# A layer norm queued two to four gate pieces sooner, half of its sums of squares on VectorE, and two output rows interleaved by weight half

## The chip, the cores and the metric

One core of one Trainium2 chip runs the whole program. The metric is the device time of one execution in microseconds (us), as the median of several runs. A profiled execution gives a trace with a record of each instruction on each engine. The engines are called PE (TensorE, the matrix engine), DVE (VectorE), ACT (ScalarE), POOL (GpSimd) and SP (SyncE, which here only issues transfers).

## The reference

The reference is one step of a streaming encoder with two layers, for a prompt of 1024 frames and 8 running streams of 16 frames each: 1152 rows of 1024 numbers, in float32. Layer 0 is attention beside a spatial gate. Layer 1, where the change lies, is this (shortened):

```
def _conv_layer(x, conv_state, norm_g, w_in, w_dw, b_dw, ln_g, ln_b, w_out):
    xn = _rmsnorm(x, norm_g)
    z = jnp.einsum('btd,de->bte', xn, w_in)
    a, b, g = jnp.split(z, [C_WIDTH, 2 * C_WIDTH], axis=-1)
    u = a * jax.nn.sigmoid(b)
    ctx = ...                       # u behind 30 earlier rows
    c = lax.conv_general_dilated(ctx, w_dw, ...) + b_dw        # depthwise, 31 taps
    c = jax.nn.silu(_layernorm(c, ln_g, ln_b)) * jax.nn.silu(g)
    y = x + jnp.einsum('btc,cd->btd', c, w_out)
    return y, ctx[:, -(CONV_WIDTH - 1):]
```

`_layernorm` subtracts the mean over the 1024 channels, divides by the root of the variance, scales and shifts. After layer 1 a last RMS norm with `final_g` gives the outputs `y_prompt` (1024 rows) and `y_sample` (128 rows).

## The kernel before

Every float32 product is made of three matmuls: each operand is split into a high part and the rest (`wh`, `wl` for weights, `yh`, `yl` for the normed input, `ch`, `cl` for the layer's result), and `mm3` (L157) adds high by high, high by rest and rest by high. `split_w` splits a piece of weights of 128x1024: a load into `raw` on SP's queue, a cast to `wh` on ACT (L145), and a subtraction to `wl` on DVE, or on the engine given as `low` (L146).

In `phase_conv` channels lie on the partitions and the 1152 rows (tokens) along the free side. Eight arrays `cT[0..7]`, each 128x1152, hold the convolution's result for 128 channels each. Most conv tiles go through memory: the result is stored in `s_c`, loaded into a `big` buffer, and copied into `cT[i]` with the bias by DVE (L1217 and L1220, inside `back`). `back` also adds up `msum`, the sum of `cT[0]` to `cT[6]`.

After the conv tiles come eight gate tiles i (0 to 7, 128 gate channels each). A gate tile has three column pieces c of 384 tokens. A piece is 24 matmuls of 128x384 (8 channel blocks by 3), then a silu on ACT into `sg[i]` (L980). Below, the pieces are numbered 3i + c, from 0 to 23.

The layer norm runs beside the gate tiles, for one column piece c at a time, in three steps:

- `norm_sum` (L1009 to L1020): two matmuls with a matrix `ones` add the channels of `msum` and `cT[7]`; ACT writes the mean into `msum` (L1011); for each of the eight blocks DVE subtracts it (L1014), ACT squares (L1016) into a buffer, and POOL adds the square to one of two sums, `ac0` and `ac1` (L1020). The squares of blocks 0 and 1 are the sums' first values; the other six go through two buffers, `sq`, used in turn.
- `norm_var` (L1028 to L1034): six narrow matmuls add each of the sums over the channels; DVE and POOL make the inverse root (L125, L126); DVE writes it on diagonals (L1034).
- `norm_apply` (L1041 to L1045): a matmul spreads it over the partitions, ACT copies it into `msum` (L1042); for each block DVE multiplies (L1044) and ACT applies scale, shift and silu (L1045).

`LN_STEPS` gives for each c the pieces behind whose last matmul these three steps are issued. The order within each engine's queue is set by the program's scheduler, which simulates the program as it is written; `issue_after` ties a step to an instruction. `ones` is written by a memset on DVE (L1002) after `back(7)`.

Behind the gate tiles DVE multiplies `cT` by `sg` (L1064, 24 operations). Then w_out's product runs over nine tiles t of 128 rows. For each tile ACT casts `ch2` from the eight `cT` (L1079), DVE subtracts to `cl2` (L1080), and PE makes two products of 24 matmuls of 128x512, one for each half of w_out's columns; DVE adds each to `x`, and a norm writes the rows out. The first half of w_out's weights is split beside the last gate tiles (the list `wo`), the second half at the start of the last stage. PE runs its queue strictly in order.

Of the kernel before, what the change touches and what calls it, by code (L numbers as in the profile page):

```python
# [11 lines left out]
F32 = mybir.dt.float32  # L12
F32R = mybir.dt.float32r
AF = mybir.ActivationFunctionType
ALU = mybir.AluOpType
# [4 lines left out]
P = 128  # L20
# [5 lines left out]
NT = 9  # L26
# [68 lines left out]
BACK = 3  # L95
HPT = 400
TAIL = 1
LN_STEPS = ((10, 13, 15), (13, 16, 18), (16, 19, 21))
LAST = (7, 4, 6, 3, 5, 2, 1, 0)
QB = 4  # L100
GB = 3
# [3 lines left out]
class Builder:  # L105
# [809 lines left out]
    def phase_conv(self):  # L915
        nc, tc, a = self.nc, self.tc, self.a
        with ExitStack() as st:
            E = st.enter_context
            pm = E(tc.tile_pool(name="pm2", bufs=3, space=PSUM, reuse_waits="tile"))
# [10 lines left out]
            cT = [cp.tile([P, TOK], F32, name=f"cT{i}") for i in range(8)]  # L930
# [42 lines left out]
            def gate_tile(i, wb):  # L973
                i2 = i % 2
                for c in range(3):
                    ts_ = slice(c * 384, (c + 1) * 384)
                    ps = pm.tile([P, 512], F32, name="mm")
                    last = self.mm3(ps[:, :384], [(x[:, i2 * P:(i2 + 1) * P], y[:, i2 * P:(i2 + 1) * P]) for x, y in wb],
                                    self.yk(c))
                    nc.scalar.activation(sg[i][:, ts_], ps[:, :384], AF.Silu)  # L980
# [24 lines left out]
            def norm_sum(c):  # L1005
                ts_ = slice(c * 384, (c + 1) * 384)
                mu = msum[:, ts_]
                ps = pl.tile([P, 512], F32, name="ln")
                nc.tensor.matmul(ps[:, :384], lhsT=ones, rhs=mu, start=True, stop=False)  # L1009
                nc.tensor.matmul(ps[:, :384], lhsT=ones, rhs=cT[7][:, ts_], start=False, stop=True)  # L1010
                nc.scalar.activation(mu, ps[:, :384], AF.Copy, scale=1.0 / D)  # L1011
                acc = [None, None]
                for i in range(8):
                    nc.vector.tensor_tensor(cT[i][:, ts_], cT[i][:, ts_], mu, ALU.subtract)  # L1014
                    sq = wk.tile([P, 384], F32, name="sq" if i > 1 else f"ac{i}", bufs=2 if i > 1 else 1)
                    nc.scalar.activation(sq, cT[i][:, ts_], AF.Square)  # L1016
                    if i < 2:
                        acc[i] = sq
                    else:
                        nc.gpsimd.tensor_tensor(acc[i % 2], acc[i % 2], sq, ALU.add)  # L1020
                ln[c] = acc

            def norm_var(c):
# [28 lines left out]
            for j in range(1, 4):  # L1052
                wb = self.split_w(wp, [a["w_in1"][:, 2 * D + j * 256:2 * D + (j + 1) * 256]], 256)
                for i2 in range(2):
                    i = 2 * j + i2
# [2 lines left out]
                        wo = [self.split_w(wp, [a["w_out1"][:, :512]], 512, p) for p in range(2)]  # L1058
            wo += [self.split_w(wp, [a["w_out1"][:, :512]], 512, p) for p in (2, 3)]
            wb = [sum(wo, [])]  # L1060
            for c in range(3):
                ts_ = slice(c * 384, (c + 1) * 384)
                for i in range(8):
                    nc.vector.tensor_tensor(cT[i][:, ts_], cT[i][:, ts_], sg[i][:, ts_], ALU.mult)  # L1064
            s3.close()
            s4.close()
            self.xstack.close()
            with ExitStack() as s2:
                wp4 = s2.enter_context(tc.tile_pool(name="wp4", bufs=4, side="right", reuse_waits="tile"))
# [4 lines left out]
                for t in range(NT):  # L1074
                    ts_ = slice(t * P, (t + 1) * P)
                    ch = wk.tile([P, 8, P], F32R, name="ch2")
                    cl = wk.tile([P, 8, P], F32R, name="cl2")
                    for i in range(8):
                        nc.scalar.copy(ch[:, i], cT[i][:, ts_])  # L1079
# [3 lines left out]
                    for i in range(2):  # L1083
                        ps = pm.tile([P, 512], F32, name="mm")
                        self.mm3(ps, [(ch[:, k], cl[:, k]) for k in range(8)], wb[i])
                        nc.vector.tensor_tensor(x[:, i * 512:(i + 1) * 512], x[:, i * 512:(i + 1) * 512], ps, ALU.add)
                    yo = wk.tile([P, D], F32, name="yo")
                    if t == NT - 1:
                        self.norm_out(a["y_sample"].rearrange("b q d -> (b q) d"), yo, x, gb)
                        continue  # L1090
                    self.norm(yo, x, gb)
                    nc.sync.dma_start(out=a["y_prompt"][0, ts_, :], in_=yo)
            self.wstack.close()

    def conv_tile(self, i, wb, pm, ub, cv, chan, wdw, scr, same, hooks, late):
# [154 lines left out]
```

## Time and profile before

| | |
|---|---|
| median of 3 runs | 1223.09 us (1223.04 to 1224.46) |
| profiled execution | 1223.68 us, span 1221.9 us |
| mean granted clock of PE | 0.979 of full speed |
| ACT busy | 456.8 us (37%), 1065 instructions |
| POOL busy | 340.7 us (28%), 510 instructions |
| gate pieces 7 to 23 and norm steps | about 1027 to 1108 us |
| last gate matmul begins | 1108.18 us |
| first w_out matmul begins | 1113.00 us |

Times in the trace count from the span's start. The profiled execution's own time is 1.8 us longer than its span. Busy time counts an engine's instructions and not its waits; a record's length can be longer than the slot that it takes, since an engine begins an instruction before the one ahead has ended. What a stretch costs is read from starts.

### The profile page before, as it was taken

To read this page: it belongs to the slowest core of one execution; us is meant where nothing else is said; L and a number is where in the kernel's file an instruction comes from. 1 tells how busy PE (TensorE), PEld (TensorE's weight loads), DVE (VectorE), ACT (ScalarE), POOL (GpSimd) and SP (SyncE) were. 2 spreads that over 40 slices of the span, in tenths; PEclk is the share of its full clock that TensorE was granted. 3 is DMA by queue.
4 is the path that set the end of the run, shared out by engine and by line. 5 is a ranking of instruction groups with operands and counts; after the bars stand their busy time and mean duration, and the time that the engine had idled before them with its cause. 6 is when DMAs were issued, how large, how long until landed. Compare 5 with 4: busy or idle time off the path is not lost. (4 is left out here: it accounts for less than half of the span.)

```text
span 1221.9 us, 20908 instructions
## 1 busy us (share of the span) xinstructions
PE 1156.0 (95%) x7886; PEld 1024.1 (84%) x7886; DVE 731.6 (60%) x1560; ACT 456.8 (37%) x1065; POOL 340.7 (28%) x510
## 2 busy tenths in 40 slices
PE   6999999999989998679999999999999999998997
PEld 4878998899989997457777677899999899996886
DVE  4420225678788878766556444698999711377443
ACT  4431223445454545555444334312121222365221
POOL 2233223334434435413322231212131220350000
PEclk9999999999989998879999999999999999998999
DMA  8453435324132313867767635333332442113331
GB/s 302 110 169 91 144 118 172 107 71 121 46 89 78 108 50 105 301 214 242 258 226 255 192 125 190 92 91 96 93 96 90 140 134 84 35 35 104 104 104 69
DMA packets 125365, 160.33 MB, mean 131 GB/s; under 512 B 16514, under 2 KB 87194, under 8 KB 125257
## 3 DMA queue, kind: packets, MB, share of 16 engines
q1 hardware_dynamic: 109344, 106.95, 28.5%
q0 software_dynamic: 15776, 51.79, 12.9%
q8 instruction: 62, 1.02, 0.3%
q14 instruction: 39, 0.31, 0.1%
q10 hardware_dynamic: 144, 0.26, 0.1%
HBM read 119.41 MB, written 40.00 MB: 130 GB/s over the span
## 5 line engine op out<-in xcount | busy, mean ns | idle before, releaser
L157 PE MATMUL mm<-yh,wh 128*128 128x384 f32 x576 | 196.5, 341 | 3.3 <-ACT sb L1133 2.5
L157 PE MATMUL mm<-yl,wh 128*128 128x384 f32 x576 | 193.9, 337 | 0.5 <-issue 0.5
L157 PE MATMUL mm<-yh,wl 128*128 128x384 f32 x576 | 193.8, 338 | 0.3 <-DVE wl L146 0.2
L157 PE MATMUL mm<-wh,xh 128*128 128x384 f32 (+1 forms) x504 | 185.4, 369 | 2.5 <-DVE sg L468 1.4
L157 PE MATMUL mm<-wl,xh 128*128 128x384 f32 (+1 forms) x504 | 184.5, 366 | 0.9 <-DVE wl L146 0.9
L157 PE MATMUL mm<-wh,xl 128*128 128x384 f32 (+1 forms) x504 | 183.7, 364 | 0.0
L146 DVE TENSOR_TENSOR wl<-raw,wh 128x1024 fp32r<-128x1024 f32 (+1 forms) x72 | 84.3, 1178 | 104.7 <-ACT wh L145 102.7
L1173 DVE SCALAR_TENSOR_TENSOR cT<-u,cc,cT 128x128 f32<-128x128 f32 (+1 forms) x180 | 141.3, 843 | 1.0
L157 PEld LDWEIGHTS mm<-yh,wh 128*128 128x128 f32 x576 | 108.7, 189 | 6.2 <-issue 2.8
L157 PEld LDWEIGHTS mm<-yh,wl 128*128 128x128 f32 x576 | 108.6, 189 | 2.0 <-DVE wl L146 0.9
L157 PEld LDWEIGHTS mm<-yl,wh 128*128 128x128 f32 x576 | 108.7, 189 | 1.1 <-issue 0.7
L157 PEld LDWEIGHTS mm<-wh,xh 128*128 128x128 f32 x504 | 95.7, 190 | 13.3 <-DVE sg L468 1.4
L157 PEld LDWEIGHTS mm<-wl,xh 128*128 128x128 f32 x504 | 95.9, 190 | 10.5 <-DVE wl L146 1.8
L157 PEld LDWEIGHTS mm<-wh,xl 128*128 128x128 f32 x504 | 95.7, 190 | 8.7 <-DVE xl L170 0.3
L145 ACT CAST wh<-raw 128x1024 fp32r<-128x1024 f32 (+1 forms) x72 | 71.8, 1001 | 73.0 <-PE mm L157 30.9
L126 POOL TENSOR_TENSOR rr<-pw,mhalf 128x1 f32<-128x1 f32 x59 | 33.0, 559 | 200.3 <-DVE pw L125 190.8
L559 ACT ACTIVATE e<-S,nm 128x512 f32<-128x512 f32 (+5 forms) x96 | 55.1, 579 | 42.1 <-DVE nm L554 26.4
L157 PE MATMUL out<-wh,ch 128*128 128x512 f32 x144 | 59.9, 416 | 2.0 <-DVE xr L845 1.2
L157 PE MATMUL mm<-wh,ch 128*128 128x512 f32 x144 | 57.1, 397 | 4.5 <-ACT ch L1079 4.5
L551 DVE TENSOR_REDUCE nm<-S 128x1 f32<-128x512 f32 (+5 forms) x96 | 52.5, 551 | 12.6 <-PE S L546 11.9
L777 DVE TENSOR_TENSOR vl<-vraw,vh 128x1024 fp32r<-128x1024 f32 x32 | 43.2, 1351 | 26.8 <-ACT vh L776 26.6
L157 PE MATMUL out<-wh,cl 128*128 128x512 f32 x144 | 58.8, 408 | 0.0
(282 smaller groups left out, 2300.6 us busy)
## 6 DMA issues: line engine op xcount, KB each, us to landing
raw<-in_cache_k SPq DMA_DIRECT2D x32, 512.0 KB, 4.4
vraw<-in_cache_v POOLq DMA_DIRECT2D x32, 512.0 KB, 5.7
raw<-in_w_in SPq DMA_DIRECT2D x24, 512.0 KB, 5.3
raw<-in_w_out SPq DMA_DIRECT2D x16, 512.0 KB, 5.0
raw<-in_w_in SPq DMA_DIRECT2D x32, 256.0 KB, 4.0
raw<-in_w_in SPq DMA_DIRECT2D x48, 128.0 KB, 2.8
s_y<-xr POOLq DMA_DIRECT2D x9, 512.0 KB, 4.7
x<-s_y SPq DMA_DIRECT2D x9, 512.0 KB, 4.3
```

The lines of the kernel that those rows point to most:

```text
L126: m = nc.gpsimd.tensor_tensor(out, v[:, :w], self.mhalf[:, :w], ALU.pow)
L145: nc.scalar.copy(h[:, :ks * n], raw[:, :ks * n])
L146: (low or nc.vector).tensor_tensor(l[:, :ks * n], raw[:, :ks * n], h[:, :ks * n].bitcast(F32), ALU.subtract)
L157: m = self.nc.tensor.matmul(out, lhsT=x, rhs=y, start=(i == 0), stop=(i == n - 1))
L551: nc.vector.tensor_reduce(nm[:, j:j + 1], s[:, :n], AX.X, ALU.max, negate=True)
L559: nc.scalar.activation(e[:, j * n:(j + 1) * n], S[j][:, :n], AF.Exp, bias=nv, accum_out=zz[:, j:j + 1])
L777: (nc.vector if i in VDVE else nc.gpsimd).tensor_tensor(vl, vr, vh.bitcast(F32), ALU.subtract)
L1173: nc.vector.scalar_tensor_tensor(dst, src, w1, dst, ALU.mult, ALU.add)
```

## The change

There are four edits. The layer norm's steps are issued behind earlier pieces. The sums of squares of odd blocks (`ac1`) are added on DVE. The multiplication by `sg` moves into gate tile 7, behind each of its pieces. In the last stage the second half's splits have their subtraction on POOL and are issued ahead of the load of `final_g`, and the products of rows 0 and 1 run in the order (0, first half), (1, first half), (0, second half), (1, second half).

```diff
-LN_STEPS = ((10, 13, 15), (13, 16, 18), (16, 19, 21))
+LN_STEPS = ((6, 9, 11), (10, 13, 15), (14, 17, 19))
...
                     with tc.issue_after(last):
                         for f in (hooks_of(8) if i < 2 else steps).get(3 * i + c, ()):
                             f()
+                    if i == 7:
+                        for k in range(8):
+                            nc.vector.tensor_tensor(cT[k][:, ts_], cT[k][:, ts_], sg[k][:, ts_], ALU.mult)
...
-                        nc.gpsimd.tensor_tensor(acc[i % 2], acc[i % 2], sq, ALU.add)
+                        (nc.vector if i % 2 else nc.gpsimd).tensor_tensor(acc[i % 2], acc[i % 2], sq, ALU.add)
...
-            for c in range(3):
-                ts_ = slice(c * 384, (c + 1) * 384)
-                for i in range(8):
-                    nc.vector.tensor_tensor(cT[i][:, ts_], cT[i][:, ts_], sg[i][:, ts_], ALU.mult)
...
+                wb.append(self.split_w(wp4, [a["w_out1"][:, 512:]], 512, low=nc.gpsimd))
                 nc.sync.dma_start(out=gb, in_=a["final_g"].partition_broadcast(P))
-                wb.append(self.split_w(wp4, [a["w_out1"][:, 512:]], 512))
...
+                rows_in(0)
+                rows_in(1)
+                for t, i in ((0, 0), (1, 0), (0, 1), (1, 1)):
+                    product(t, i)
+                rows_out(0)
+                rows_out(1)
+                for t in range(2, NT):
+                    rows_in(t)
+                    for i in range(2):
+                        product(t, i)
+                    rows_out(t)
```

`rows_in` holds the old loop's casts, subtractions and load of `x` for one tile, `product` one product and its addition to `x`, `rows_out` the norm and the store. The new lines shift the numbers: L1009, L1020 and L1044 of before are L1012, L1023 and L1047 after, and so on; the multiplication by `sg` is L986 (before L1064).

PE's queue around the first `norm_sum`. Before, its pair of matmuls stands between pieces 10 (tile 3, c = 1) and 11 (`yh1` and `yh2` are the normed input of columns 1 and 2; a name in brackets with a number, as in DVE_49, is a semaphore that the instruction waits for):

```order
L157 MATMUL mm_11255<-yl1_8100,wh_11147 128x384
L157 MATMUL mm_11255<-yh1_8099,wl_11148 128x384
L1009 MATMUL ln_11281<-msum_8270,ones_11137 128x384 [waits DVE_49,PE_49]
L1010 MATMUL ln_11281<-cT7_8269,ones_11137 128x384
L157 MATMUL mm_11315<-yh2_7982,wh_11141 128x384 [waits Activation_49]
```

and after, inside piece 7 (tile 2, c = 1), behind eleven of its matmuls:

```order
L157 MATMUL mm_11211<-yh1_8099,wh_11141 128x384 [waits Activation_49]
L157 MATMUL mm_11211<-yl1_8100,wh_11141 128x384
L157 MATMUL mm_11211<-yh1_8099,wl_11142 128x384
...
L157 MATMUL mm_11211<-yh1_8099,wh_11141 128x384
L157 MATMUL mm_11211<-yl1_8100,wh_11141 128x384
L1012 MATMUL ln_11177<-msum_8270,ones_11137 128x384 [waits DVE_49,Activation_49]
L1013 MATMUL ln_11177<-cT7_8269,ones_11137 128x384
L157 MATMUL mm_11211<-yh1_8099,wl_11142 128x384
```

The pair has moved up by three and a half pieces. DVE's queue ahead of the subtractions has the same order in both: here it is after the change.

```order
L146 TENSOR_TENSOR wl_11412<-raw_11409,wh_11411 128x1024 [waits PE_49,Activation_49]
L1236 TENSOR_SCALAR cT7_8269<-big_11089,cc_8271 128x1024 [waits DMAHW6_49]
L1239 TENSOR_SCALAR cT7_8269<-big_11089,cc_8271 128x8x8 x2
L146 TENSOR_TENSOR wl_11418<-raw_11415,wh_11417 128x1024 [waits DMAHW5_49,PE_49,Activation_49]
L1005 MEMSET ones_11137 128x128 [waits DMAHW1_49,Pool_49]
L1017 TENSOR_TENSOR cT0_8262<-cT0_8262,msum_8270 128x384 [waits DVE_49,Activation_49]
```

The memset of `ones`, on which L1012 waits, is still the last of these before the subtractions.

DVE's queue from the second column's `norm_sum` on, after the change (L1017 subtracts the mean, L1023 is DVE's share of the sums, L1047 belongs to the first column's `norm_apply`):

```order
L1017 TENSOR_TENSOR cT7_8269<-cT7_8269,msum_8270 128x384 [waits PE_49]
L146 TENSOR_TENSOR wl_11551<-raw_11548,wh_11550 128x1024 [waits PE_49,Activation_49]
L146 TENSOR_TENSOR wl_11557<-raw_11554,wh_11556 128x1024 [waits DMAHW7_49,PE_49,Activation_49]
L1023 TENSOR_TENSOR ac1_11338<-ac1_11338,sq_11345 128x384 [waits Activation_49]
L1047 TENSOR_TENSOR cT0_8262<-cT0_8262,msum_8270 128x384 [waits Activation_49]
L1047 TENSOR_TENSOR cT1_8263<-cT1_8263,msum_8270 128x384
L1047 TENSOR_TENSOR cT2_8264<-cT2_8264,msum_8270 128x384
...
L1047 TENSOR_TENSOR cT7_8269<-cT7_8269,msum_8270 128x384
L1023 TENSOR_TENSOR ac1_11338<-ac1_11338,sq_11353 128x384 [waits Activation_49]
```

Before, the same multiplications (of the third column's sums, L1044) stand like this:

```order
L1044 TENSOR_TENSOR cT0_8262<-cT0_8262,msum_8270 128x384 [waits DVE_49,Activation_49]
L1044 TENSOR_TENSOR cT1_8263<-cT1_8263,msum_8270 128x384 [waits DVE_49]
L1044 TENSOR_TENSOR cT2_8264<-cT2_8264,msum_8270 128x384 [waits DVE_49]
L1044 TENSOR_TENSOR cT3_8265<-cT3_8265,msum_8270 128x384 [waits DVE_49]
L1044 TENSOR_TENSOR cT4_8266<-cT4_8266,msum_8270 128x384 [waits DVE_49]
```

The multiplications have moved into the second column's sums, and their wait for a semaphore of DVE's own is gone.

ACT's queue at the end of the gate tiles, before the change:

```order
L145 CAST wh_11867<-raw_11865 128x1024 [waits DMAHW3_49,PE_49]
L1045 ACTIVATE cT5_8267<-cT5_8267,cc_8271 128x384 [waits DVE_49]
L980 ACTIVATE sg7_11133<-mm_11833 128x384 [waits PE_49]
L145 CAST wh_11908<-raw_11906 128x1024 [waits DMAHW4_49]
L1079 CAST ch2_11930<-cT0_8262 128x128
```

and after it:

```order
L1048 ACTIVATE cT7_8269<-cT7_8269,cc_8271 128x384 [waits DVE_49]
L980 ACTIVATE sg7_11133<-mm_11781 128x384 [waits PE_49]
L980 ACTIVATE sg7_11133<-mm_11815 128x384 [waits PE_49]
L145 CAST wh_11885<-raw_11883 128x1024 [waits DMAHW2_49,PE_49,Activation_49]
L145 CAST wh_11891<-raw_11889 128x1024 [waits DMAHW3_49,PE_49,Activation_49]
L980 ACTIVATE sg7_11133<-mm_11849 128x384 [waits PE_49]
L145 CAST wh_11907<-raw_11905 128x1024 [waits DMAHW4_49]
L1080 CAST ch2_11930<-cT0_8262 128x128
```

The last `norm_apply` (L1048) has moved ahead of gate tile 7's first silu (L980); the two casts of weights around the last silu stand where they stood.

More of the change, by code (lines that the diff above doesn't have):

```diff
@@ L1071, in phase_conv, with rows_in @@
                 gb = wk.tile([P, D], F32, name="gb", bufs=1)
+                wb.append(self.split_w(wp4, [a["w_out1"][:, 512:]], 512, low=nc.gpsimd))
                 nc.sync.dma_start(out=gb, in_=a["final_g"].partition_broadcast(P))
[L1073 to L1074 removed]
+                rows = {}
+                def rows_in(t):
                     ts_ = slice(t * P, (t + 1) * P)
@@ L1082, in phase_conv, with product, rows_out @@
                     nc.sync.dma_start(out=x, in_=self.s_y1[ts_, :])
[L1083 to L1086, printed above, removed]
+                    rows[t] = ch, cl, x
+                def product(t, i):
+                    ch, cl, x = rows[t]
+                    ps = pm.tile([P, 512], F32, name="mm")
+                    self.mm3(ps, [(ch[:, k], cl[:, k]) for k in range(8)], wb[i])
+                    nc.vector.tensor_tensor(x[:, i * 512:(i + 1) * 512], x[:, i * 512:(i + 1) * 512], ps, ALU.add)
+                def rows_out(t):
+                    x = rows[t][2]
                     yo = wk.tile([P, D], F32, name="yo")
```

4 lines of the change are left out of this document (2 added, 2 removed).

## Prediction

> **What bounds the kernel.** First the page's table of busy time, then the waits of the matrix engine (PE) after 1000 us, which is where everything in the change lies, and then the last pieces of the chain that ended last (start, length, what).
>
> ```profile
> PE 1156.0 (95%) x7886; PEld 1024.1 (84%) x7886; DVE 731.6 (60%) x1560; ACT 456.8 (37%) x1065; POOL 340.7 (28%) x510
> ...
> PE mm L157 <- ACT ch L1079: 4.5, 1, 4.5
> PE mm L157 <- DVE wl L146: 0.7, 1, 0.7
> ...
> 1115.36 99.09 PE mm L157 x429
> ```
>
> PE is busy 95% of the span, and the chain's last long piece is PE's alone. So a microsecond that PE stands still after 1000 us comes out as a microsecond of the end, and work of the other engines costs nothing while PE has matmuls. Between 1000 us and the last gate matmul PE waits for no engine; its waits are both at the seam where the gate tiles end and the w_out product begins. So the change can gain only at that seam, and can lose wherever the earlier steps make PE wait. The seam comes next: PE's records (start, us, line, tile, and in brackets the idle time before), then windows (length, PE busy, instructions, granted clock, DMA share, GB/s).
>
> ```profile
> 1108.18 0.34 PE L157 MATMUL mm<-yh,wl 128*128 128x384 f32 x1
> 1113.00 0.79 PE L157 MATMUL mm<-wh,ch 128*128 128x512 f32 x1 [4.48 <-ACT ch L1079]
> ...
> 1118.83 0.39 PE L157 MATMUL mm<-wh,ch 128*128 128x512 f32 x1
> 1119.05 0.39 PE L157 MATMUL mm<-wl,ch 128*128 128x512 f32 x1
> ...
> 1108.44:1111.86 3.42, 0.08 (x1) 1.00 0.66 213
> 1111.86:1115.27 3.41, 1.65 (x3) 0.50 0.72 263
> 1115.27:1118.68 3.41, 3.32 (x8) 0.50 0.81 263
> 1118.68:1122.10 3.42, 3.42 (x17) 1.00 0.08 31
> ```
>
> The last gate matmul's slot ends at 1108.36 (0.17 a slot). Eleven matmuls start from 1113.00 to before 1118.83 (x3 and x8 in the windows). At full clock, from 1118.83 on, one takes a slot of 0.227 (0.39 is its own length, which overlaps the next). So 10.5 us from 1108.36 to 1118.83 did work of 11 slots, 2.5 us. The seam loses 8.0 us. Two things make it: idle time, 5.2 us, and two windows at half clock, which follow a window in which PE did almost nothing.
>
> **The clock's price.** The granted clock changes on a grid of 3.41 us. Two earlier places show what it takes.
>
> ```profile
> 492.64 0.66 PE L417 MATMUL tr<-cst,raw 128*128 128x128 f32 x4 [2.21 <-DVE KT L418]
> ...
> 490.63:494.04 3.41, 1.05 (x7) 1.00 0.86 310
> 494.04:497.46 3.42, 3.42 (x18) 0.50 0.75 238
> 975.32:978.73 3.41, 1.81 (x84) 1.00 0.45 159
> 978.73:982.14 3.41, 3.41 (x107) 1.00 0.02 5
> ```
>
> A window with PE busy for 0.31 of it was followed by one at half clock; one with 0.53 was not. I take one half as the limit. A half-clock window costs 1.7 us, half of its length. So a gap of over 1.7 us can cost its length and 1.7 more, if it falls into one window.
>
> **Part A, norm_sum of the first column piece, four gate pieces sooner.** In the new order its two matmuls over `ones` stand behind 11 matmuls of gate piece 7 instead of behind piece 10. They wait for VectorE (DVE), whose queue ahead of them has not moved: the copies of the last conv tile (L1217, L1220), a weight split, and then the memset of `ones`.
>
> ```profile
> 1029.71 1.20 DVE L1217 TENSOR_SCALAR cT<-big,cc 128x1024 f32<-128x1024 f32 x1 [6.29 <-DMA big<-s_c]
> 1030.84 0.44 DVE L1220 TENSOR_SCALAR cT<-big,cc 128x64 f32<-128x64 f32 x2
> 1031.21 1.21 DVE L146 TENSOR_TENSOR wl<-raw,wh 128x1024 fp32r<-128x1024 f32 x1
> 1032.39 0.17 DVE L1002 MEMSET ones<- 128x128 f32 x1
> ...
> 1027.32 0.33 PE L157 MATMUL mm<-yh,wh 128*128 128x384 f32 x1
> ...
> 1029.22 0.33 PE L157 MATMUL mm<-yh,wl 128*128 128x384 f32 x1
> ```
>
> 1027.32 is piece 7's first matmul; 11 slots later, at 1029.23, PE reaches the moved pair. The memset ends at 1032.56, because the DMA that feeds L1217 lands at 1029.71. PE therefore stands 3.3 us. That DMA hangs on the convolution, which the change does not touch, and behind the pair PE's whole gate work is queued in order. The clock: the grid (1108.44 less 23 windows) has an edge at 1029.9, so of the window to 1033.35 PE works some 0.8 us, under a quarter; the next is at half clock, 1.7. If the grid lies otherwise, two windows may share the gap and neither falls. Part A costs 3.3 to 5.0; I take 5.0.
>
> **Part B, the sums of squares.** Of the 18 additions nine go from POOL to DVE. On DVE one costs a slot of 0.48 (eight L1014 in 3.84 below). Nine are 4.3 us, and four weight splits of 1.15 leave DVE, both beside PE work. What matters is how POOL fares beside DVE. Here are POOL's additions and one small power operation, with what DVE did meanwhile.
>
> ```profile
> 1049.01 3.94 POOL L1020 TENSOR_TENSOR ac<-ac,sq 128x384 f32<-128x384 f32 x1 [46.64 <-ACT sq L1016]
> ...
> 1049.26 0.55 DVE L1014 TENSOR_TENSOR cT<-cT,msum 128x384 f32<-128x384 f32 x1
> 1049.73 2.35 DVE L146 TENSOR_TENSOR wl<-raw,wh 128x1024 fp32r<-128x1024 f32 x2
> ...
> 1052.92 3.92 POOL L1020 TENSOR_TENSOR ac<-ac,sq 128x384 f32<-128x384 f32 x4
> ...
> 1080.70 3.83 DVE L1014 TENSOR_TENSOR cT<-cT,msum 128x384 f32<-128x384 f32 x8
> 1080.86 4.39 POOL L126 TENSOR_TENSOR nm<-pw,mhalf 128x3 f32<-128x3 f32 x1 [6.39 <-DVE pw L125]
> ...
> 1071.37 1.33 POOL L1020 TENSOR_TENSOR ac<-ac,sq 128x384 f32<-128x384 f32 x1
> ...
> 1070.65 2.47 DVE L1044 TENSOR_TENSOR cT<-cT,msum 128x384 f32<-128x384 f32 x2 [5.11 <-ACT msum L1042]
> ```
>
> An addition alone takes 0.98 (four in 3.92). The one at 1049.01 took 3.94 and ended 0.9 after DVE's run of two-input operations ended at 1052.08: it had not begun before. The power operation likewise waited out eight L1014. At 1071, beside L1044, it was otherwise: POOL's addition took 1.33 and two L1044 took 2.47 instead of 1.2, so they alternated. The difference in the program is that each L1044 waits for a semaphore of DVE's own, and L1014 and the splits do not. In the new order the multiplications (now L1047) carry no such wait either, as the L1014 of before. So a run of them shuts POOL out.
>
> For the second column piece DVE's queue is then one such run: eight subtractions, two splits, one addition, eight multiplications of the first column's norm_apply, 3.8 + 2.3 + 0.5 + 3.8 = 10.4 us. POOL's first addition of that column is asked for inside it.
>
> ```profile
> 1043.96 0.81 PE L1009 MATMUL ln<-msum,ones 128*128 128x384 f32 x2
> 1044.60 0.81 PE L1010 MATMUL ln<-cT,ones 128*128 128x384 f32 x2
> ...
> 1045.97 3.84 DVE L1014 TENSOR_TENSOR cT<-cT,msum 128x384 f32<-128x384 f32 x8 [13.42 <-ACT msum L1011]
> 1046.62 0.52 ACT L1016 ACTIVATE ac<-cT 128x384 f32<-128x384 f32 x1 [0.69 <-DVE cT L1014]
> ```
>
> From norm_sum's first matmul: DVE begins after 2.0 (1045.97 less 1043.96), its run ends after 12.4, POOL's first addition after 13.3. The two `sq` buffers make the later squares wait for it, so square, addition, square, addition follow: 2 x (0.52 + 0.98), after 16.3, and 0.2 for the hand-overs. PE comes to norm_var after 72 gate matmuls of 0.173 and three wide matmuls of 0.64, 14.4. It stands 2.1 us; the clock's 1.7 comes with it about three times in five, and I take it: 3.8. The bounds: POOL gets in early and nothing is lost, 0; or POOL's third addition too is shut out by the gate multiplications that now follow in DVE's queue, another 2, so 5.8.
>
> The Trainium skill ("SBUF — State Buffer", section "SBUF: two separate sides") says that VectorE's two-input operations and GpSimd share one port pair as a lock, which whoever starts first holds for one instruction. By it POOL would get in at the next instruction's end, and the sum would lack B (the first rival). The rows of 1.33 and 2.47 agree with that, those of 3.94 and 4.39 do not: there POOL waited out two to eight instructions.
>
> **Part C, the third column.** Its last addition now stands on DVE behind seven multiplications (7 x 0.47 = 3.3) with the split that opens the last gate tiles behind it; PE waits for both. The square that it needs comes late itself, so I take 0.5, between 0 and 3.3.
>
> **The seam after the change.** All norm_apply steps and nearly all gate multiplications (L986, before L1064) are over by the last gate matmul. ScalarE (ACT) still has in its queue a weight cast whose buffer the last gate piece frees, the last silu, a second cast, and then the first `ch2` cast, for which PE waits.
>
> ```profile
> 1109.80 1.03 ACT L145 CAST wh<-raw 128x1024 fp32r<-128x1024 f32 x1
> ...
> 1111.35 0.47 ACT L980 ACTIVATE sg<-mm 128x384 f32<-128x384 f32 x1
> 1111.72 1.03 ACT L145 CAST wh<-raw 128x1024 fp32r<-128x1024 f32 x1
> 1112.65 0.70 ACT L1079 CAST ch<-cT 128x128 fp32r<-128x128 f32 x3
> ```
>
> Slots of 0.94 + 0.37 + 0.93 and a cast of 0.3: 2.6 us idle (5.2 before). One window, not two, then runs at half clock: 1.7. The seam loses 4.3 instead of 8.0, a gain of 3.7; 5.4 if the clock holds, 8.0 if the seam closes. Interleaving rows 0 and 1 puts 48 matmuls (10.9 us) ahead of the first use of w_out's second half, so its four splits, now on POOL, are hidden even at 2.4 us each, the length of an operation of that size there:
>
> ```profile
> L180 POOL TENSOR_TENSOR yn<-yn,gb 128x1024 f32<-128x1024 f32 x8 | 19.1, 2392 | 10.1 <-ACT yn L179 10.1
> ```
>
> The swapped loads on SP's queue and the second `x` load land long before the additions after 24 matmuls. The norm of row 0 comes later, beside row 2's product: nothing. The end after the last matmul does not change.
>
> **Sum.** 5.0 + 3.8 + 0.5 - 3.7 = +5.6 on the profiled execution's 1223.68, 1229.3. That execution lies 0.59 above the median of the runs, 1223.09, so 1228.7.
>
> **Rivals.** First: POOL gets in between DVE's operations, B is 0. For it speak the rows at 1071; against it those at 1049 and 1080, whose unmarked operations are the kind that the new order has. 5.0 + 0.5 - 3.7 = +1.8: 1224.9. Chance 0.19.
>
> Second, the other side: the seam closes wholly, because the casts come early enough that `ch2` is ready by the last gate matmul. It decides if ACT has the first cast done at the slot's end; then 8.0 is gained, and with B and C at nothing 5.0 - 8.0 = -3.0, 1220.1. Against it: the cast that waits for the last gate matmul stands ahead of `ch2` in ACT's queue. Chance 0.08.
>
> Third: the gaps of 2 to 3 us never lower the clock. 3.3 + 2.1 + 0.5 - 5.4 = +0.5: 1223.6. The row with 2.21 idle at 492.64 and its half-clock window speak against it. Chance 0.08. The Trainium skill ("TensorE: Matmul & The Clock Gate", section "Why this matters for your kernels") warns only of PE gaps over some 3 us, which would give this rival's time; the trace's clock fell with a gap of 2.21.
>
> Fourth: at the seam POOL's first split takes the port before the `cl2` subtractions, and PE's third matmul waits out most of its 2.4: 2.2 more, 1230.9. For it: POOL's split is asked for before the `cl` of row 0. Chance 0.12.
>
> **Chances and range.** My forecast, A and B with the smaller seam, has 0.53; its own range is 1227 (B without the clock) to 1231 (a longer B). Within 0.2% of the median (2.45 us, about what a measurement here can tell from no change) lie the first rival, near the edge, and the third; faster is the second. With a little of the first over the edge: faster 0.08, same 0.24, slower 0.68. The range takes the first, third and fourth in and reaches to B's upper bound: 1223.0 to 1233.0.
>
> **What would show it.** A: a wait of L1012 for DVE of about 3.3 near 1029, then a window at 0.50. B: a POOL addition of several us at about 1056 to 1064, ending just after DVE's multiplications, and PE's L1031 waiting about 2 for POOL near 1067. The seam: 2.6 idle before the first w_out matmul, released by `ch2`, and one window at half clock. I am wrong if `ones` is there by 1029, if POOL's additions all stay near 1.0 to 1.4, or if the seam's wait is gone.

## The result, and the profile after

The changed kernel is slower: 1230.45 us median (1229.41 to 1233.0, 6 runs) against 1223.66 for the kernel before on the same chip, a ratio of 1.0056 with a 95% interval of 1.0044 to 1.0069. The forecast was 1228.7, in a range of 1223.0 to 1233.0. The profiled execution took 1229.75 us with a span of 1228.0, 6.1 more than the span before.

PE's waits after 1000 us (line, who was waited for, total, times, longest), of the changed kernel:

```profile
PE ln L1012 <- DVE ones L1005: 3.4, 1, 3.4
PE mm L157 <- ACT ch L1080: 2.5, 1, 2.5
PE ln L1031 <- POOL ac L1023: 1.9, 1, 1.9
PE mm L157 <- DVE cl L1081: 1.9, 1, 1.9
PE ln L1032 <- DVE ac L1023: 0.5, 1, 0.5
PE mm L157 <- DVE wl L146: 0.3, 1, 0.3
```

The busy shares of the page say nothing: they are the same within a point (PE 94% of the span after 95%). The waits say more. Before there were two, at the seam, of 5.2 us. Now there are six, of 10.5 us, and the first, third, fifth and sixth stand in the gate tiles, where PE had not waited for any engine.

The two stages can be read from three records of PE in each trace: the first matmul of gate piece 7, the last gate matmul, and the last matmul of w_out. For the changed kernel:

```profile
1026.52 0.33 PE L157 MATMUL mm<-yh,wh 128*128 128x384 f32 x1
...
1115.74 0.34 PE L157 MATMUL mm<-yh,wl 128*128 128x384 f32 x1
...
1220.11 0.39 PE L157 MATMUL mm<-wh,cl 128*128 128x512 f32 x1
```

From piece 7 to the last gate matmul are 89.22 us (before: 1108.18 less 1027.32, 80.86), a loss of 8.4. From there to the last matmul are 104.4 us (105.9 before), a gain of 1.5. Piece 7 itself began 0.8 earlier, which has nothing to do with the change. 8.4 - 1.5 - 0.8 gives the 6.1 of the span. So the two stages together lost 6.9, and 0.8 of it was made up by chance.

The first wait. DVE's rows, and PE's:

```profile
1029.07 1.11 DVE L1236 TENSOR_SCALAR cT<-big,cc 128x1024 f32<-128x1024 f32 x1 [6.45 <-DMA big<-s_c]
1030.46 1.22 DVE L146 TENSOR_TENSOR wl<-raw,wh 128x1024 fp32r<-128x1024 f32 x1
1031.65 0.17 DVE L1005 MEMSET ones<- 128x128 f32 x1
...
1031.96 1.26 PE L1012 MATMUL ln<-msum,ones 128*128 128x384 f32 x2 [3.37 <-DVE ones L1005]
...
1028.89:1032.30 3.41, 0.34 (x1) 1.00 0.07 28
1032.30:1035.71 3.41, 3.41 (x9) 0.51 0.50 156
```

PE stands from 1028.6 until the memset is done; a window with PE busy for a tenth is followed by one at half clock.

The second column's sums, DVE and POOL and then PE:

```profile
1053.12 3.84 DVE L1017 TENSOR_TENSOR cT<-cT,msum 128x384 f32<-128x384 f32 x8 [3.75 <-ACT msum L1014]
1056.87 2.36 DVE L146 TENSOR_TENSOR wl<-raw,wh 128x1024 fp32r<-128x1024 f32 x2
1059.14 0.56 DVE L1023 TENSOR_TENSOR ac<-ac,sq 128x384 f32<-128x384 f32 x1
1059.61 3.84 DVE L1047 TENSOR_TENSOR cT<-cT,msum 128x384 f32<-128x384 f32 x8
...
1056.20 8.12 POOL L1023 TENSOR_TENSOR ac<-ac,sq 128x384 f32<-128x384 f32 x1 [7.54 <-issue]
1064.95 1.01 POOL L1023 TENSOR_TENSOR ac<-ac,sq 128x384 f32<-128x384 f32 x1 [0.63 <-ACT sq L1019]
...
1067.64 0.38 PE L1031 MATMUL ln<-ones,ac 128*128 128x1 f32 x2 [1.92 <-POOL ac L1023]
...
1063.02:1066.43 3.41, 2.69 (x16) 1.00 0.04 14
1066.43:1069.85 3.42, 2.21 (x13) 1.00 0.01 2
```

DVE runs without a gap from 1053.12 to 1063.45. POOL's addition is on record as 8.12 us long and busy; it ends 0.9 after the run. An addition alone takes 1.01, in the next row. The clock did not fall: the gap lies across the edge of two windows, which are 0.79 and 0.65 busy.

The seam:

```profile
1118.60 0.50 PE L157 MATMUL mm<-wh,ch 128*128 128x512 f32 x1 [2.52 <-ACT ch L1080]
1121.17 0.79 PE L157 MATMUL mm<-wh,cl 128*128 128x512 f32 x1 [1.85 <-DVE cl L1081]
...
1118.42 2.54 POOL L146 TENSOR_TENSOR wl<-raw,wh 128x1024 fp32r<-128x1024 f32 x1 [22.86 <-ACT wh L145]
1118.67 5.48 DVE L1081 TENSOR_TENSOR cl<-cT,ch 128x128 fp32r<-128x128 f32 x16
...
1121.05:1124.46 3.41, 3.29 (x8) 0.50 1.03 398
```

POOL's first split began 0.25 before DVE's `cl2` subtractions and lasted until 1120.96; PE's first matmul over `cl` began 0.2 later. So the seam has 2.5 idle for `ch2`, 1.85 for `cl2` and one half-clock window of 1.7, some 6 us. The stage gained 1.5 on the 8.0 of before, which puts the loss at 6.5.

### The profile page after: what moved, and what is told of

It reads as the page before. It is cut to its first block, busy times and chain, and to the rows that moved or that the text cites. A ratio compares the mean times of both kernels' runs of the same rounds, so it can differ in the third digit from the quotient of the medians.

```text
span 1228.0 us, 20895 instructions
## 1 busy us (share of the span) xinstructions
PE 1157.6 (94%) x7886; PEld 1025.7 (84%) x7886; DVE 734.8 (60%) x1565; ACT 456.0 (37%) x1065; POOL 342.1 (28%) x505
## 5 line engine op out<-in xcount | busy, mean ns | idle before, releaser
L146 DVE TENSOR_TENSOR wl<-raw,wh 128x1024 fp32r<-128x1024 f32 (+1 forms) x68 | 79.6, 1176 | 105.3 <-ACT wh L145 102.7
L157 PEld LDWEIGHTS mm<-wl,xh 128*128 128x128 f32 x504 | 96.3, 191 | 10.5 <-DVE wl L146 1.8
```

The source lines that it names most:

```text
L146: (low or nc.vector).tensor_tensor(l[:, :ks * n], raw[:, :ks * n], h[:, :ks * n].bitcast(F32), ALU.subtract)
L157: m = self.nc.tensor.matmul(out, lhsT=x, rhs=y, start=(i == 0), stop=(i == n - 1))
```

## The experiments

All times of stages come from the three PE records named above, one profiled execution each. The ratio is that of the runs to those of the kernel before on the same chip, with its 95% interval. The start of piece 7 moved between 1025.5 and 1033.7 from one execution to the next (e9 aside, whose first wait stands ahead of it), on code that no kernel here changes, so the stages are the sharper measure. They hold the half-clock windows that the execution happened to have, some 1.7 us each, so the table gives their number, with PE's waits in the gate stage.

| kernel | gate, us | of it waits | w_out, us | half-clock windows, gate and w_out | ratio to before |
|---|---|---|---|---|---|
| before | 80.9 | 0 | 105.9 | 0, 2 | 1 |
| the change | 89.2 | 6.2 | 104.4 | 1, 1 | 1.0056 [1.0044, 1.0069] |
| e1: first column at 8, 10, 12 | 81.9 | 1.0 | 105.4 | 0, 2 | 1.0000 [0.9985, 1.0015] |
| e2: multiplications read PSUM | 87.0 | 4.4 | 105.3 | 1, 2 | 1.0058 [1.0036, 1.0080] |
| e3: second half split on DVE | 90.5 | 5.9 | 103.3 | 2, 1 | 1.0043 [1.0025, 1.0061] |
| e4: all sums on POOL | 94.1 | 6.6 | 104.2 | 4, 1 | 1.0077 [1.0057, 1.0098] |
| e5: old steps | 85.7 | 3.1 | 104.8 | 1, 2 | 1.0030 [1.0011, 1.0049] |
| e6: all sums on DVE | 88.7 | 4.8 | 105.5 | 2, 2 | 1.0040 [1.0019, 1.0061] |
| e7: rows not interleaved | 91.9 | 5.7 | 104.0 | 3, 1 | 1.0080 [1.0055, 1.0105] |
| e8: better steps, all on DVE | 80.5 | 0 | 102.3 | 0, 1 | 0.9956 [0.9940, 0.9973] |
| e9: `ones` written early | 91.5 | 5.3 | 104.2 | 3, 1 | 1.0051 [1.0032, 1.0071] |
| e10: the steps alone | 96.4 | 7.0 | 102.9 | 5, 1 | 1.0091 [1.0062, 1.0120] |
| e11: e8 with half the sums on POOL | 80.4 | 0 | 102.0 | 0, 1 | 0.9941 [0.9922, 0.9960] |

In every row the gate stage is the 80.9 of before, PE's waits and 1.7 for each half-clock window, within 0.5 us. So no larger cost is hidden in that stage. The gate stage of the change, e3 and e7 is the same code with nearly the same waits; its 89.2, 90.5 and 91.9 differ by their one, two and three half-clock windows. A difference of one or two windows between single profiles therefore need not be an effect of an edit. The intervals of e2, e3, e4, e5, e6, e7, e9 and e10 all overlap that of the change. So the runs alone tell these kernels from the change barely or not at all, and what is said of them below rests on the waits in their profiles.

The main theory is that of the prediction: two stalls in the gate tiles that the earlier steps make (one for `ones`, one for POOL shut out by DVE), and a smaller gain at the seam. The main rival is that the work moved to DVE makes the loss.

### e1: the first column two pieces later

```diff
-LN_STEPS = ((6, 9, 11), (10, 13, 15), (14, 17, 19))
+LN_STEPS = ((8, 10, 12), (10, 13, 15), (14, 17, 19))
```

> The changed kernel with the first column's steps behind pieces 8, 10 and 12 instead of 6, 9 and 11. Theory (two stalls and the seam): norm_sum now reaches PE after the memset of ones (about 1031.8), so the 3.4 us wait of L1012 and its half-clock window (1.7) are gone, 5.1; in return norm_var of the second column comes to PE earlier against POOL, whose addition stays shut out, so L1031's wait for POOL grows from 1.9 to about 3 and may cost a half-clock window. Net 2 to 4 us faster than the changed kernel, about 1227. Rival (the extra work on VectorE makes the loss, the wait for ones is covered by later slack): within 1 us of the changed kernel, 1230.

PE's waits of e1, then POOL's first addition of the second column with what DVE did:

```profile
PE mm L157 <- ACT ch L1080: 2.5, 1, 2.5
PE mm L157 <- DVE cl L1081: 1.9, 1, 1.9
PE ln L1032 <- DVE ac L1023: 1.0, 1, 1.0
...
1059.48 2.25 POOL L1023 TENSOR_TENSOR ac<-ac,sq 128x384 f32<-128x384 f32 x1 [4.19 <-issue]
...
1059.66 1.22 DVE L146 TENSOR_TENSOR wl<-raw,wh 128x1024 fp32r<-128x1024 f32 x1
1062.32 0.56 DVE L1023 TENSOR_TENSOR ac<-ac,sq 128x384 f32<-128x384 f32 x1 [1.44 <-ACT sq L1019]
```

The wait for `ones` is gone as expected. The wait for POOL is gone too, which was not expected. With `norm_apply` one piece later DVE's run stops after a split at 1060.88 and DVE waits 1.44 for a square; in that pause POOL's addition ran and ended at 1061.73. So one row of the table removed 7.3 us of the 8.4 lost in the gate tiles, and the kernel is as fast as before. The rival falls: DVE did the same additions and multiplications.

### e2: norm_apply's multiplications read PSUM

```diff
-                nc.scalar.copy(mu, ps[:, :384])
                 for i in range(8):
-                    nc.vector.tensor_tensor(cT[i][:, ts_], cT[i][:, ts_], mu, ALU.mult)
+                    nc.vector.tensor_tensor(cT[i][:, ts_], cT[i][:, ts_], ps[:, :384], ALU.mult)
```

> The changed kernel with norm_apply's multiplications (L1047) reading the spread root straight from PSUM instead of ACT's copy in msum, so that they have one input in SBUF and not two; nothing else is changed. Theory (POOL is shut out by runs of VectorE operations with two SBUF inputs): POOL's addition at 1056 ends when the two splits and the addition behind them end, near 1060.6 and not at 1064.3; its 8.1 us become about 4.4, and L1031's wait for POOL of 1.9 is gone: 1 to 3 us faster than the changed kernel, since a wait of the next gate tile for its cast may take up to 2 back. Rival (POOL waits for any run of VectorE, or for something else): the addition still lasts about 8 us and the time is the same within 1 us.

```profile
1058.04 2.77 POOL L1023 TENSOR_TENSOR ac<-ac,sq 128x384 f32<-128x384 f32 x1 [7.55 <-issue]
1059.85 3.80 DVE L1046 TENSOR_TENSOR cT<-cT,ln 128x384 f32<-128x384 f32 x8
...
PE ln L1012 <- DVE ones L1005: 2.6, 1, 2.6
PE mm L157 <- ACT ch L1079: 2.5, 1, 2.5
PE mm L157 <- DVE cl L1080: 1.9, 1, 1.9
PE mm L157 <- ACT sg L980: 1.8, 1, 1.8
```

The eight multiplications (L1046 here) take 3.80 as before, but POOL's addition now ends at 1060.81, in their midst, 0.9 after the last operation with two inputs in SBUF. So it is two-input runs that shut POOL out, and an operation with one input in PSUM does not. The run that POOL had to wait out was shorter here as well: the queue has one split and no addition ahead of the multiplications, where the changed kernel has two splits and an addition. The wait for POOL is gone, and a new one of 1.8 for a silu stands in gate tile 6, where the changed kernel waited 0.5 and 0.3: the gate stage is 2.2 shorter, and the runs do not tell it from the changed kernel. Most of the wait taken away was replaced by a later one.

### e3: w_out's second half split on VectorE

```diff
-                wb.append(self.split_w(wp4, [a["w_out1"][:, 512:]], 512, low=nc.gpsimd))
+                wb.append(self.split_w(wp4, [a["w_out1"][:, 512:]], 512))
```

> The changed kernel with the four subtractions of w_out's second half back on VectorE. Theory (at the seam POOL's first split holds VectorE's cl2 subtractions for its 2.5 us, PE's wait of 1.85): that wait goes, but VectorE's own first split of 1.15 then stands ahead of cl2, as before the change, for a wait of about 1. Net 0.5 to 1 us faster than the changed kernel, about 1229.7. Rival (cl2 is late for another reason, such as the last gate multiplication): the wait stays at 1.85 or grows, and the time is the same or 1 us slower.

```profile
PE mm L157 <- DVE cl L1081: 0.8, 1, 0.8
```

PE's wait for `cl2` fell from 1.9 to 0.8, and the w_out stage from 104.4 to 103.3: as forecast. So POOL's split cost the seam about 1.1. The gate stage, whose code is the same, was 1.2 longer in this execution, with one more half-clock window, and the ratio's interval overlaps that of the change.

### e4: all sums on POOL

```diff
-                        (nc.vector if i % 2 else nc.gpsimd).tensor_tensor(acc[i % 2], acc[i % 2], sq, ALU.add)
+                        nc.gpsimd.tensor_tensor(acc[i % 2], acc[i % 2], sq, ALU.add)
```

> The changed kernel with all sums of squares on POOL again, at the new steps. Theory (POOL is shut out beside VectorE's runs, and the early steps leave no time for it): six additions of 1.0 instead of three must follow each run of VectorE, so norm_var's wait for POOL appears in two columns, about 2 and 1 to 2 us with half-clock windows, and gate tiles' casts come late: 3 to 7 us slower than the changed kernel, 1233 to 1237. Rival (the additions on VectorE are the loss): faster than the changed kernel by 1 us or more.

```profile
1055.06 11.76 POOL L1023 TENSOR_TENSOR ac<-ac,sq 128x384 f32<-128x384 f32 x5 [6.54 <-issue]
```

Five additions take 11.8 us. PE waits 2.0 for POOL in one column only, where two were expected, and 1.4 for a gate tile's cast, with two half-clock windows behind each. The gate stage is 4.8 longer, but its waits are only 0.4 longer in all: the rest is three more half-clock windows, and e7 has two more than the change with unchanged gate code. The runs' interval overlaps that of the change. So the profile points to a help from the half of the sums on DVE at these steps, and does not show it. The wait of 3.1 for `ones` had no half clock behind it here.

### e5: the old steps

```diff
-LN_STEPS = ((6, 9, 11), (10, 13, 15), (14, 17, 19))
+LN_STEPS = ((10, 13, 15), (13, 16, 18), (16, 19, 21))
```

> The changed kernel with the old steps for the layer norm, 10-13-15, 13-16-18, 16-19-21; the other edits stay. Theory: L1012's wait for ones is gone, and so is the run of VectorE that shuts POOL out of the second column; but the last norm_apply again runs at the end of the gate tiles, and now the gate multiplications with it, so the next gate tile's weight split on VectorE comes about 3 us late and the seam is as wide as in the kernel before. From gate piece 7 to the last gate matmul 83 to 86 us (89.2 in the changed kernel, 80.9 before), the w_out stage 105 to 106, and in all 1 to 4 us faster than the changed kernel. Rival (the early steps are good in themselves and the new sums and splits make the loss): slower than the changed kernel.

```profile
PE mm L157 <- ACT ch L1080: 3.5, 1, 3.5
PE mm L157 <- DVE wl L146: 2.4, 1, 2.4
PE mm L157 <- ACT sg L980: 0.8, 1, 0.8
```

Nearly as forecast: no wait for `ones` or POOL, a split 2.4 late and a gate stage of 85.7; the w_out stage, 104.8, is a little shorter than expected. The other edits without the steps are slower than the kernel before (0.1% to 0.5%), so the steps are not the whole loss. By the median they are less slow than the change, but the two intervals overlap a little.

### e6: all sums on VectorE

```diff
-                        (nc.vector if i % 2 else nc.gpsimd).tensor_tensor(acc[i % 2], acc[i % 2], sq, ALU.add)
+                        nc.vector.tensor_tensor(acc[i % 2], acc[i % 2], sq, ALU.add)
```

> The changed kernel with all sums of squares on VectorE, none on POOL. Theory: L1031's wait for POOL of 1.9 us is gone with POOL's additions; the nine more additions of 0.5 make VectorE's queue 4.5 us longer, and the split for the next gate tile comes up to 2 us late in the third column. L1012's 3 us wait stays. From piece 7 to the last gate matmul 86.5 to 89 us, in all 0 to 2.5 us faster than the changed kernel. Rival (additions on VectorE are what lengthens the gate stage): 1 us or more slower than the changed kernel.

The wait for POOL is gone, and a wait of 1.9 for a weight split on DVE has come. Gate stage 88.7, with two half-clock windows. As in e2, one wait for another.

### e7: rows 0 and 1 one after the other

```diff
-                for t, i in ((0, 0), (1, 0), (0, 1), (1, 1)):
+                for t, i in ((0, 0), (0, 1), (1, 0), (1, 1)):
```

> The changed kernel with rows 0 and 1 not interleaved: (0, first half), (0, second half), (1, first half), (1, second half). POOL's four splits end about 10.5 us after the first ch2 cast (1131.15 in the changed kernel's trace, and each takes 2.5 to 2.9). Theory: row 0's second product now asks for them 24 matmuls sooner, 5.4 us, so PE waits for POOL once or twice, about 1.5 us in all, with a half-clock window at worst 3 us: 1 to 3 us slower than the changed kernel in the w_out stage (104.4). Rival (the interleaving does nothing, since the weights are there anyway): the same w_out stage within 0.5 us.

The forecast missed: PE never waited for POOL's splits, and the w_out stage is 104.0, no longer than with the interleaving. The weights come in time either way. The runs have a higher median, but their interval overlaps that of the change. What the profile loses beyond the change lies in the gate stage, which is the same code: there the clock fell twice where it had not in the changed kernel. PE's record and the windows of e7:

```profile
1074.33 0.38 PE L1031 MATMUL ln<-ones,ac 128*128 128x1 f32 x2 [1.92 <-POOL ac L1023]
...
1072.68:1076.09 3.41, 1.76 (x11) 1.00 0.01 2
1076.09:1079.51 3.42, 3.42 (x12) 0.50 0.00 0
...
1096.57:1099.99 3.42, 2.56 (x18) 1.00 0.00 0
1099.99:1103.40 3.41, 3.41 (x12) 0.50 0.53 162
```

The first wait is the 1.92 of the changed kernel, but here it lies within one window, which is 0.52 busy. So the same wait costs 1.9 us or 3.6, depending on where the grid lies. The second fall is behind the third column's waits of 0.5 and 0.3, which the changed kernel has too: here both lie in one window, and half clock followed though it was 0.75 busy.

### e8: a version that avoids the stalls

```diff
-LN_STEPS = ((6, 9, 11), (10, 13, 15), (14, 17, 19))
+LN_STEPS = ((8, 11, 13), (11, 14, 16), (14, 17, 19))
...
-                        (nc.vector if i % 2 else nc.gpsimd).tensor_tensor(acc[i % 2], acc[i % 2], sq, ALU.add)
+                        nc.vector.tensor_tensor(acc[i % 2], acc[i % 2], sq, ALU.add)
...
-                wb.append(self.split_w(wp4, [a["w_out1"][:, 512:]], 512, low=nc.gpsimd))
...
                 rows_in(1)
+                wb.append(self.split_w(wp4, [a["w_out1"][:, 512:]], 512))
```

> A version that avoids the stalls found: steps 8-11-13, 11-14-16, 14-17-19, all sums of squares on VectorE, w_out's second half on VectorE and split behind the casts of rows 0 and 1, the rest as in the changed kernel. Theory: no wait of L1012 (ones is written by then), none for POOL, no late split, so from piece 7 to the last gate matmul about 80.5 to 81.5 us as in the kernel before (80.9); at the seam one cast fewer ahead of ch2, so about 1.6 us idle and then about 0.9 for cl2 instead of 2.5 and 1.85, w_out stage 101 to 103 us (105.9 before). In all 3 to 5 us faster than the kernel before. Rival (VectorE, which holds all of it, becomes the bound at the seam or delays a gate tile): as long as the kernel before or longer.

```profile
PE mm L157 <- ACT ch L1079: 1.6, 1, 1.6
PE mm L157 <- DVE cl L1080: 0.6, 1, 0.6
```

Only the seam's two waits are left, 2.2 us against 5.2 before. Gate 80.5, w_out 102.3, in all 0.44% faster than the kernel before, about 5 us. The gate stage is as short as before, so the gain is at the seam: 3.0 less idle and one half-clock window fewer. The early steps and the later place of the second half's splits both bear on it, and this run does not part them.

### e9: `ones` written early

The two lines stand ahead of the gate tiles; the buffer is one that the conv tiles no longer use.

```diff
-            ones = wk.tile([P, P], F32, name="ones", bufs=1)
+            ones = self.ut[0][:, :P]
             nc.vector.memset(ones, 1.0)
```

> The changed kernel with ones in a buffer of its own that is written some 15 us earlier, so that no matmul waits for its memset; the steps stay. The scheduler now puts norm_sum's pair right behind piece 6, 11 matmuls sooner. Theory (the step itself comes too early: cT[7] is copied from a DMA that lands late, and behind it came the memset): the wait moves from L1012 to L1013, which needs cT[7]; its copy ends about 4.0 us after piece 7 would begin, so PE waits 3 to 3.4 there, with a half-clock window as before, and the time is that of the changed kernel within 1.5 us; from piece 7 to the last gate matmul, with that wait counted in, 87 to 90. Rival (the memset behind the weight split is the cause): 3 to 5 us faster than the changed kernel.

```profile
1034.03 0.81 PE L1012 MATMUL ln<-msum,utmp 128*128 128x384 f32 x2
1037.35 0.91 PE L1013 MATMUL ln<-cT,utmp 128*128 128x384 f32 x2 [2.51 <-DVE cT L1236]
```

The wait moved to the pair's second matmul, which needs `cT[7]`, 2.5 us instead of 3.4. But the edit moved the pair too: it now stands ahead of piece 7, eleven matmuls or 1.9 us sooner. The gate stage of the table counts from the pair, 1034.03: it is 91.5, more than the 87 to 90 expected, with two half-clock windows in the sums that the changed kernel's execution did not have. The runs are as slow as those of the change. So the step at its new place comes ahead of its data, which come by DMA. How long the pair would wait for `cT[7]` at the changed kernel's place is not measured. An estimate from that kernel's rows is 0.9: the copy of `cT[7]` ends at 1030.18, and PE stops at 1028.6 and would have L1012's 0.65 to do first. By it, some 2.5 of the 3.4 belong to the split and the memset behind the copy.

### e10: the steps alone

The kernel before with the new table.

```diff
-LN_STEPS = ((10, 13, 15), (13, 16, 18), (16, 19, 21))
+LN_STEPS = ((6, 9, 11), (10, 13, 15), (14, 17, 19))
```

> The kernel before with the new table of steps alone: all sums on POOL, gate multiplications after the gate tiles, splits and rows as before. Theory: L1012's wait of 3 us with its half-clock window, POOL shut out in the second column (2 us) and late in the third, casts late behind it: from piece 7 to the last gate matmul 92 to 96 us (80.9 before, 89.2 in the changed kernel), the w_out stage 103 to 105, in all 9 to 14 us slower than the kernel before. So the steps are the loss, and the sums on VectorE give a part of it back. Rival (the steps are harmless, and the sums on VectorE make the loss): within 3 us of the kernel before.

```profile
PE ln L1009 <- DVE ones L1002: 3.0, 1, 3.0
PE mm L157 <- ACT ch L1079: 2.5, 1, 2.5
PE ln L1028 <- POOL ac L1020: 2.0, 1, 2.0
PE mm L157 <- DVE wl L146: 1.2, 2, 0.8
PE mm L157 <- ACT wh L145: 1.1, 1, 1.1
```

The gate stage grows by 15.5, a little beyond what was expected: 7.0 of waits and five half-clock windows. The w_out stage shrinks by 3.0, and the runs are 0.6% to 1.2% slower, by the median more than with the whole change. The steps alone bring both stalls and the smaller seam. That the sums on DVE give a part back is likely from this run and e4, but not shown: the other edits differ here too, and the intervals overlap.

### e11: e8 with half of the sums on POOL

To e8 come the change's split of the sums and the reading of PSUM from e2.

```diff
-                        nc.vector.tensor_tensor(acc[i % 2], acc[i % 2], sq, ALU.add)
+                        (nc.vector if i % 2 else nc.gpsimd).tensor_tensor(acc[i % 2], acc[i % 2], sq, ALU.add)
...
-                nc.scalar.copy(mu, ps[:, :384])
...
-                    nc.vector.tensor_tensor(cT[i][:, ts_], cT[i][:, ts_], mu, ALU.mult)
+                    nc.vector.tensor_tensor(cT[i][:, ts_], cT[i][:, ts_], ps[:, :384], ALU.mult)
```

> The better version (steps 8-11-13, 11-14-16, 14-17-19; w_out's second half late and on VectorE) with the sums of squares halved between VectorE and POOL as in the change, and norm_apply's multiplications reading PSUM, so that they have one input in SBUF. Theory (POOL's additions do no harm where VectorE's runs leave it the port and the steps leave time): no wait for POOL of over 0.5 us, from piece 7 to the last gate matmul 80.5 to 82, as fast as the better version within 1.5 us. Rival (any sum on POOL beside these runs makes PE wait): 2 us or more slower than the better version.

As expected: no wait for POOL, the same stages as e8, and 0.4% to 0.8% faster than the kernel before. Where the sums run no longer matters when the steps leave time for them and the multiplications leave POOL its port; the two were not tried apart here.

## Why the prediction was right, point by point

**Direction and size.** The forecast was +5.6 on the profile before; the span grew by 6.1, and the medians are 6.8 apart. Where the gate tiles lose time, and by what, was right; that the size came so close was partly luck. Two misses nearly offset each other: the clock at part B, forecast 1.7 too high, and the seam's gain, forecast 2.2 too high. The stages together lost 6.9, and the 0.8 by which piece 7 happened to begin earlier brought the span back to 6.1.

**Part A** was forecast at 5.0 (3.3 and 1.7 for the clock) and measured at 3.4 and one half-clock window: right. e1 shows that it goes with the step's place. The clock's share hangs on the grid, as the prediction said: in e4 a wait of 3.1 for `ones` lay across two windows and no half clock followed. The prediction set the wait on the memset, the last of what is late. The load of `cT[7]` is late too: with the memset out of the way and the pair 1.9 sooner, e9 waits 2.5 for it.

**Part B** was forecast at 2.1 and 1.7. The wait was 1.9, by the mechanism named: 8.1 us for an addition of 1.0, ended 0.9 after DVE's run, and the addition freed in e2 by taking one SBUF input away. The step that failed is the clock's share: the gap lay across two windows and the clock did not fall. It fell behind the same wait in e7 and e9, and not in e3. The prediction gave it three chances in five and then counted it in full.

By the rule of the Trainium skill that the prediction drew on ("SBUF — State Buffer", section "SBUF: two separate sides"), the lock is held for one instruction; an addition that waits out a dozen instructions of DVE, most of them begun after it was asked for, is not what that leads one to expect. The trace agrees with another part of the same sentence, that a VectorE operation holds the pair against GpSimd with two SBUF inputs: with one in PSUM, in e2, POOL got in. What decides between DVE's next operation and a waiting POOL was not measured apart.

**Part C** was forecast at 0.5; the two waits are 0.5 and 0.3. The sum had no clock term for them. In e3, e7 and e9 one half-clock window stood behind these waits, 1.7 more; that the changed kernel's profiled execution has none is luck.

**The limit of one half** for the clock does not hold as a rule. In the trace before, the window from 692.02 was 0.55 busy and was followed by half clock, while the one that the prediction shows, 0.53 busy, was not; in e7 windows of 0.52 and 0.75 were. What decides was not found.

**The seam** is the term most wrong: a gain of 3.7 forecast, 1.5 measured. The wait for `ch2` (2.5 for 2.6) and the one half-clock window came as worked out, but the second of these hangs on the grid: in e1, e2 and e6, with the same two waits at the seam, two windows ran at half clock, and the stage of 105.3 to 105.5 gained only 0.4 to 0.6. What was left out of the sum is the fourth rival, POOL's split ahead of `cl2`, which the prediction gave 0.12: it took place, for 1.85 of the 2.2 priced. e3 takes it away and finds 0.8 in its stead, DVE's own split, which the sum had not counted either. So of the 2.2 missed, 1.1 is the price of the split on POOL over that on DVE, 0.8 the wait that DVE's own split would have made, and 0.3 stays open.

**The interleaving** was costed at nothing because the splits are hidden. They are hidden, but e7 shows them hidden without it too.

**The rivals.** That POOL gets in between DVE's operations did not happen at these steps; that the seam closes did not; that the clock never falls did not, though for part B it held.

What stays open: how much of the loss in the runs' median is the clock's. One half-clock window more or less is 1.7 us of the 6.8 between the medians, and the windows can be counted only in the profiled executions. The mean granted clock of each run gives an estimate: the changed kernel's six runs have 0.977 on average (0.975 to 0.980), the runs of the kernel before that were made beside the experiments 0.978 to 0.979. A thousandth of 1228 us is 1.2 us, so 1 to 2 us of the 6.8.

## What to carry to other kernels

A step moved earlier in a strictly ordered queue must find its operands ready at its new place: look up when the last of them lands, DMA included, before moving it, and when one operand is made early, look at when the next one comes. On DVE a long run of operations with two SBUF inputs stopped POOL throughout, so work shared between the two was safe here only where DVE paused or read one input from PSUM. Settle the place of the steps first and the sharing of work afterwards: here the place of one column's steps gave 7 us, and at the later steps sharing the sums made no difference to the time.

## What the runs showed of the hardware that was not expected

- POOL's record counts the time shut out as busy: 8.12 us for an addition of 1.01. A long POOL record beside a full DVE is a wait.
- The lock works the other way round too: while a POOL split of 128x1024 ran, 2.54 us, DVE's first `cl2` subtraction (0.28 us each later on) took 2.45 us and ended just after it.
- A DVE operation that reads one input from PSUM was as fast as from SBUF (eight in 3.80 against 3.84) and left POOL its port.
- The busy share of one window of 3.41 us did not alone decide the clock of the next. The same gap of 1.92 us was followed by half clock where it lay in one window (0.52 busy, e7) and not where it lay across two (0.79 and 0.65, the changed kernel). But two gaps of 0.5 and 0.3 in one window that was 0.75 busy were followed by half clock too (e7).
